# A trunk layer's output projection: four token tiles against eight weight chunks, or a block of seven half-size products

## The chip, the cores and the metric

The kernel runs on one core of one Trainium2 chip, in one launch. The metric is the device time of a run in microseconds; lower is better. Each engine has its own instruction queue: PE (matrix products, with its weight loads PEld), DVE (vector), ACT (scalar), POOL (GpSimd) and SP (issue of DMAs). POOL issues DMAs too, the accumulating ones among them.

## The reference

A two-layer encoder trunk on 512 tokens of width 1024, in float32. Cut to the token sublayer, where the change lies:

```python
for i in range(DEPTH):                                   # DEPTH = 2
    proj = x @ w_in[i]
    ...
    merged = sigmoid(gate_a) * (ya @ w_branch_a[i]) + sigmoid(gate_b) * (yb @ w_branch_b[i])
    y = merged @ w_out[i]                                # 512 x 1024 by 1024 x 1024
    x = layer_norm(DEEPNORM_ALPHA * x + y, ln1_g[i], ln1_b[i])
    ffn = conv_glu_ffn(x, w_up[i], conv_w[i], conv_b[i], w_down[i])
    ple = sigmoid(x @ w_ple_gate[i]) * (p[i] @ w_ple_proj[i])
    x = layer_norm(DEEPNORM_ALPHA * x + ffn + ple, ln2_g[i], ln2_b[i])
```

`layer_norm` subtracts the mean, multiplies by the reciprocal root of the variance plus 1e-5, then by a gain and adds a shift per channel.

## The kernel before

**Precision.** Every float32 operand of a matmul is split into a high part and a low part (`split`, line 753: ACT casts the high part, DVE subtracts it to get the low one). `mm3` issues three matmuls for one product: high by high, high by low, low by high. Weights come in packed chunks of 128 x 1024 (0.5 MB): an SP DMA into a raw buffer, then the split. `Stream` (line 870) holds the order in which chunks are used.

**Products in blocks of seven.** Most large products are already done as 2 x 2 blocks with seven half-size products instead of eight, named a, c, t1, t2, d, t3, t4. The weight sums that this needs are made by accumulating DMAs that POOL issues into the raw buffer (`Stream.add`); `block_items` (line 771) lists the chunks of a block: which chunk starts each buffer (`src`), which one is added to it (`plus`), and which item takes the buffer over (`nxt`). `vg_sums` (line 1345) makes the sums t1, t2, d, t3 of the activations: for each, two DVE operations of 128 x 512 form it, and ACT and DVE split it.

**The stage around the change,** in both layers alike:

- The merge (line 1884): for each of eight output blocks m, a product of the attention branch (bank gt) is multiplied by its gate, the other branch (gb) is added, both on DVE, and the result is split into `mt[m]`, channel-major, 512 tokens wide.
- The residual x is in four token tiles `xn` of 128 x 1024. In layer 1 it is the previous layer's normalised but unscaled output; `x_scale` (line 1729) multiplies it by the gain and adds the shift, eight DVE operations of 1024.
- The projection, `proj_ln` (line 1149, called in line 1940): the left column half of all four token tiles over eight K pieces (bank gn), each tile's result added to ALPHA times xn and its statistics taken; then the right half, in which the last four chunks are kept (`RESIDENT`) and the tiles are finished one after another. `ln_tile` (line 1140) normalises a tile with two DVE operations of 1024, which apply gain and shift; the reciprocal root is a tiny POOL operation (`rstd_of`).
- `done1(t)` (line 1922) turns a finished tile to channel-major: eight PE transposes (bank tr), copies by ACT into `xf`, and after every second tile the split into `x1t`. Tile t - 1 is turned behind tile t's matmuls; the last one at the mark T of the next stage.
- The next stage, `pg` (line 2155), runs the gate of the per-layer embedding as a block of seven (a, c, ...), mixed with blocks of the up-projection (0a, 0c, ...), in the order `PG`. It needs the turned tiles. `ple_gate` adds ALPHA times xn to the buffer R later; for two tiles ACT scales xn and a POOL DMA adds it.
- At the layer boundary the second layer norm is done in another way: `out_pair` (line 2375) turns two tiles that are normalised only, and ACT applies gain and shift per channel while it copies them out of PSUM.

**The order of the work.** From `VG_PLAN` in each layer to the last down segment, nothing is issued in program order except PE. `Program` records every operation; `_jobs`, `_dues` and `_order` model durations (`_costs`), due times and buffers, and fix the order of the other engines' queues and of the buffers; `_best` (called in `emit`) repeats this 12 times, raises the priority of the work that PE waits for in the model, and keeps the best order. The buffers are 30 units of 128 x 1024 shared by everything, 3 raw buffers, 3 pairs for split weights, 6 temporaries, 8 PSUM banks.

Of the kernel before, what the change touches and what calls it, by code (L numbers as in the profile page):

```python
# [9 lines left out]
F32 = mybir.dt.float32  # L10
# [31 lines left out]
XN_AT = (0, 0, 0, 0)  # L42
# [6 lines left out]
RESIDENT = {(l, c) for l in range(DEPTH) for c in range(68, 72)}  # L49
# [4 lines left out]
SENT = ((20, 24), (24, 32), (32, 36), (44, 52))  # L54

# [25 lines left out]
ROUNDS = 12  # L81
# [359 lines left out]

def _best(jobs, rounds=None):

    best, part = None, {}
    for j in jobs:
        j.boost = 0.0
    rounds = rounds or ROUNDS
    for r in range(rounds + 1):
        if r == rounds:
            if not part:  # L450
                break
            for j in jobs:
                if j.plan in part:
                    j.boost = part[j.plan][1][j]
# [3 lines left out]
        if end >= 1e9:  # L458
            for j in jobs:
                j.boost *= 0.6  # L460
            continue
        free, raise_, cost, now = 0.0, {}, {}, 0
        ends = {}
        for j, _ in order:
            ends.setdefault(round(j.done, 2), []).append(j)
        for j in sorted((j for j, _ in order if j.eng == "tensor"), key=lambda j: (j.start, j.seq)):
            gap, cur = j.start - free, j
            free = max(free, j.start + j.dur)
            now = j.plan or now
            cost[now] = cost.get(now, 0.0) + max(gap, 0.0)  # L470
            if gap < 0.08 or not j.plan:
                continue
            for _ in range(14):
                last = max(cur.after, key=lambda a: (a.done, a.seq), default=None)
                if last is None or cur.eng == "tensor" and cur.start - last.done > 0.3:
                    near = [x for d in range(-30, 1) for x in ends.get(round(cur.start + d / 100, 2), ()) if x.eng != "tensor"]
                    last = near[-1] if near and cur.eng == "tensor" else None
                if last is None or last.eng == "tensor":
                    break
                cur = last  # L480
                raise_[cur] = max(raise_.get(cur, 0.0), gap)
        for p, c in cost.items():
            if p and (p not in part or c < part[p][0]):
                part[p] = c, {j: j.boost for j in jobs if j.plan == p}
        if r == rounds:
            break
        for j, g in raise_.items():
            j.boost += 0.6 * g + 0.3
    for j, (a, b) in best[2].items():
        j.start, j.done = a, b  # L490
    return best[:2]
# [208 lines left out]
def trunk(tc, wpack, x_nat, x_tr, head, p_tr, rpb, decay, ln_par, ln_col, conv, cos_t, sin_t, dist, xi_d, zd, mask, ident_d, out):  # L700
# [5 lines left out]
    with ExitStack() as es:  # L706
# [50 lines left out]
        class Item:  # L757
# [7 lines left out]
            def __init__(self, kind, src, width, pool=None, plus=None, own=None):  # L765
                self.kind, self.src, self.width, self.pool, self.plus, self.own = kind, src, width, pool, plus, own
                self.raw = self.hl = None
                self.nxt = self.early = self.block = None
                self.sent = kind == "w" and any(a <= src[1] < b for a, b in SENT)

        def block_items(pos, held, early, n=2):
# [3 lines left out]
            for kind, src, plus in (("a", "a", None), ("c", "c", None), ("t1", None, "b"), ("t2", None, "d"),  # L775
                                    ("d", "d", None), ("t3", "b", "d"), ("t4", None, "c")):
                for j in range(n):
# [8 lines left out]
                    out.append(it)  # L786
            return out
# [82 lines left out]
        class Stream:  # L870


            def __init__(self):
                self.seq = []
                for l in range(DEPTH):
                    plain = lambda c: self.seq.append(Item("w", (l, c, 0, 1024), 1024, pool=up if (l, c) in RESIDENT else None))
# [17 lines left out]
            def add(self, it):  # L894
                l, c, o, w = it.plus
# [66 lines left out]
            def planned(self, it, pools=None):  # L962
# [31 lines left out]
                if it.nxt is not None:  # L994
                    it.nxt.raw = raw
                    self.add(it.nxt)
                prog.early = early
                return it.hl

            def raw_of(self, it):  # L1000
# [15 lines left out]
                if it.plus is not None:  # L1016
                    self.add(it)
# [86 lines left out]
        def gemm_n_tok(lh, nchunk, pss, first):  # L1104

            w = [ws.get(ahead=nchunk - 1 - c) for c in range(first, nchunk)]
            for t in range(4):
                if t >= len(pss):
                    pss.append(bank("gn"))
                for c in range(first, nchunk):  # L1110
                    gn_part(pss[t], lh, w[c - first], c, t, nchunk)
                yield t
# [36 lines left out]
        def proj_ln(lh, nchunk, z, add, g, b, done, follow):  # L1149

            st = [sp.tile([P, 2, 6], F32, tag="bn", name=nm("bn")) for _ in range(4)]

            def half(t, cb, ps):
                zz = z[t][:, cb * 512:(cb + 1) * 512]
                add(zz, ps)
                nc.vector.bn_stats(st[t][:, cb, :], zz)


# [1444 lines left out]
```

## Time and profile before

| | |
|---|---|
| time of three runs, us | 1654.0, 1654.13, 1655.08 (median 1654.13) |
| span of the profiled execution, us | 1652.4 |
| PE busy, us | 1639.2 (99%) |
| PE weight loads busy, us | 1461.2 (88%) |
| DVE busy, us | 1310.2 (79%) |
| ACT busy, us | 1001.6 (61%) |
| POOL busy, us | 276.9 (17%) |
| granted TensorE clock | 0.999 |
| DMA moved | 352.84 MB, mean 214 GB/s |
| first and last projection matmul of layer 0 and 1 | from 401.2 us to 1268.0 us |

The span runs from the first to the last instruction of one execution; the page gives no other time of it, and the runs' median lies 1.7 us above it. In rows of a group, x384 counts instructions and the two numbers behind the bar are busy us and mean ns of one; rows of one tile give min/median/max ns. Timelines give the start in us, then the duration, then engine, operation, and out<-in by tile names. All tensor operations carry line 264, where the recorded program is issued, so groups are told apart by their tiles: gn with mt is the projection, gt the merge's branch products, tr the transposes, lo<-raw the weight splits, rstd the reciprocal root.

### The profile page before, as it was taken

Reading aid. Unit: us, or ns where it says so; the run is one execution under the profiler, and the core shown is the slowest. Engines: PE = TensorE matmul, PEld = TensorE weight load, DVE = VectorE, ACT = ScalarE, POOL = GpSimd, SP = SyncE. Lnnn points to the kernel's source line nnn. Section 1 sums busy time; section 2 is a strip of 40 time slices with the busy share of each in tenths; the row PEclk is TensorE's granted clock in tenths of the full one; section 3 lists DMA queues with packets and bytes.
Section 4 is the critical chain, followed back from the end, with each engine's and each line's share of the span. In section 5 each row is a group of like instructions: output and inputs, shape, how many; then the busy total and the mean of one; then the engine's idle time right before and its main releaser. Section 6 shows DMA issues by size and latency. Waiting matters only on the chain.

```text
span 1652.4 us, 25561 instructions
## 1 busy us (share of the span) xinstructions
PE 1639.2 (99%) x9765; PEld 1461.2 (88%) x9765; DVE 1310.2 (79%) x1963; ACT 1001.6 (61%) x1495; POOL 276.9 (17%) x328
## 2 busy tenths in 40 slices
PE   9999999999999999999999999999999999999997
PEld 7889999888889898898888899998888898988986
DVE  6757999786878968768894579987689799687687
ACT  6665668953567556456484557788445674563564
POOL 1211113200211111112011102121002111111113
PEclk9999999999999999999999999999999999999999
DMA  8996669865699798888589657787755997989874
GB/s 306 270 245 172 154 159 220 202 180 194 167 298 244 196 282 201 245 252 205 182 253 248 166 143 184 187 202 181 208 214 170 288 267 203 261 187 276 230 173 128
DMA packets 104827, 352.84 MB, mean 214 GB/s; under 512 B 11904, under 2 KB 16512, under 8 KB 104704
## 3 DMA queue, kind: packets, MB, share of 16 engines
q0 software_dynamic: 41040, 147.34, 45.7%
q1 hardware_dynamic: 63664, 203.86, 33.7%
q8 instruction: 77, 1.26, 0.3%
q14 instruction: 46, 0.38, 0.1%
HBM read 323.89 MB, written 25.69 MB: 212 GB/s over the span
## 4 chain that ended last, share of the span: by engine, by line
PE 92%; DVE 4%; ACT 1%; DMA 1%; issue 1%; POOL 0%; DVEq 0%; POOLq 0%; ACTq 0%
PE u L264 30%; PE gt L264 23%; PE v L264 16%; PE gn L264 9%; PE w L264 7%; PE o L264 1%; PE x L264 1%; DVE lo L264 1%; PE ns L264 1%; PE na L264 1%; PE pt L264 1%; DMA gb_scr<-p 1%; PE tr L264 1%; DVE t L264 1%; DVE R L264 0%
## 5 line engine op out<-in xcount | busy, mean ns | idle before, releaser
L264 DVE TENSOR_TENSOR lo<-rawa,hi 128x1024 fp32r<-128x1024 f32 (+1 forms) x198 | 235.0, 1196 | 80.6 <-ACT hi L264 71.6
L264 POOL DMA_DIRECT2D rawa<-in_wpack x150 | 134.2, 911 | 955.5 <-DVE lo L264 750.1
L264 ACT CAST hi<-rawa 128x1024 fp32r<-128x1024 f32 (+1 forms) x198 | 202.4, 1032 | 104.2 <-DMA rawa<-in_wpack 85.2
L264 DVE TENSOR_TENSOR lo<-raw,hi 128x1024 fp32r<-128x1024 f32 (+1 forms) x159 | 191.0, 1205 | 38.3 <-ACT hi L264 38.1
L264 PE MATMUL gt<-x1t,hi 128*128 128x512 f32 x640 | 197.4, 390 | 0.0
L264 ACT CAST hi<-raw 128x1024 fp32r<-128x1024 f32 (+1 forms) x159 | 164.5, 1040 | 50.4 <-PE gn L264 14.7
L264 PEld LDWEIGHTS gt<-x1t,hi 128*128 128x128 f32 x640 | 118.8, 188 | 23.6
L264 PE MATMUL gt<-x1t,lo 128*128 128x512 f32 x320 | 124.5, 389 | 0.0
L264 PE MATMUL v<-sh,hi 128*128 128x256 f32 x288 | 81.9, 284 | 0.0
L264 PE MATMUL u<-sh,hi 128*128 128x256 f32 x288 | 81.8, 284 | 0.0
L264 PE MATMUL u<-xt,hi 128*128 128x256 f32 x448 | 81.7, 284 | 0.0
L264 PE MATMUL u<-sh,lo 128*128 128x256 f32 x288 | 81.5, 283 | 0.0
L264 PE MATMUL v<-sh,lo 128*128 128x256 f32 x288 | 81.5, 283 | 0.0
L264 PE MATMUL u<-sl,hi 128*128 128x256 f32 x288 | 81.5, 283 | 0.0
L264 PE MATMUL v<-sl,hi 128*128 128x256 f32 x288 | 81.5, 283 | 0.0
L264 ACT ACTIVATE uh<-u 128x512 f32<-128x512 f32 x60 | 35.7, 595 | 75.5 <-PE u L264 75.4
L264 PE MATMUL gn<-hi,mt 128*128 128x512 f32 x256 | 80.3, 391 | 0.0
L264 PE MATMUL gt<-ybt,hi 128*128 128x512 f32 x256 | 79.8, 393 | 0.0
L264 ACT ACT_TABLE_LOAD x49 | 62.9, 1283 | 18.5 <-DVE gg L264 9.7
L264 PE MATMUL v<-hi,sh 128*128 128x512 f32 x184 | 71.8, 390 | 0.1
L264 PE MATMUL v<-lo,sh 128*128 128x512 f32 x184 | 71.6, 389 | 0.0
L264 PE MATMUL v<-hi,sl 128*128 128x512 f32 x184 | 71.6, 389 | 0.0
(302 smaller groups left out, 4875.4 us busy)
## 6 DMA issues: line engine op xcount, KB each, us to landing
raw<-in_wpack SPq DMA_DIRECT2D x155, 512.0 KB, 6.8
rawa<-in_wpack POOLq DMA_DIRECT2D x144, 512.0 KB, 7.7
rawa<-in_wpack SPq DMA_DIRECT2D x48, 512.0 KB, 6.8
rawt<-in_wpack SPq DMA_DIRECT2D x48, 512.0 KB, 6.0
rawt<-in_wpack POOLq DMA_DIRECT2D x48, 512.0 KB, 9.8
hi<-in_wpack POOLq DMA_DIRECT2D x40, 512.0 KB, 7.1
lo<-in_wpack POOLq DMA_DIRECT2D x40, 512.0 KB, 6.4
sx<-s_scr SPq DMA_DIRECT2D x32, 512.0 KB, 9.4
```

Source lines behind the costliest of these rows:

```text
L264: r = o.call(*[real(x) for x in o.a], **{k: real(v) for k, v in o.k.items()})
```

## The change

The projection becomes a block of seven products over token halves, K halves and column halves, in the order `WO` = a, c, t1, t2, d, t3, t4a, T0, t4b (t4 is done in two halves, one token tile each; T0 turns tiles 0 and 1 between them). `vg_sums` makes the activation sums from the merged blocks; the first-half blocks `mt[0..3]` are split for the first 256 tokens only. Results are added into xn as they come, the first time with ALPHA times xn.

The chunks of w_out go through `block_items` with `mates`: t1, t2 and t3 get their weight sums by a POOL addition of 1024 columns from another raw buffer of the block (t3, d, d), and t3's buffer is summed once more behind d; t4's sum stays an accumulating DMA. Chunks are listed for this block and `RESIDENT` goes.

The merge's addition of the other branch, layer 1's `x_scale`, and gain and shift of layer norm 1 are POOL operations. `normed` only subtracts the mean and scales by the root, one DVE operation; `turned` (the boundary's code, now shared) applies gain and shift per channel by ACT, with columns from a new small input; the POOL operations make the scaled token-major xn for the later residual, from gain and shift that ACT has multiplied by ALPHA, so that the later scaling by ALPHA goes. At the mark T, tiles 2 and 3 are turned together. `_best` makes 60 rounds instead of 12: 12 that raise priorities as before, now for each of the two planned regions apart, then random variations of the best found, with a fixed seed.

```diff
-XN_AT = (0, 0, 0, 0)
+XN_AT = ("xn", "xn", "xn", "xn")
-RESIDENT = {(l, c) for l in range(DEPTH) for c in range(68, 72)}
+WO = ("a", "c", "t1", "t2", "d", "t3", "t4a", "T0", "t4b")
-ROUNDS = 12
+ROUNDS = 60
+WALK = 12
+SEED = 1
...
+            if mates:
+                of = lambda kind: [o for o in out if o.kind == kind]
+                for t1, t2, d, t3 in zip(of("t1"), of("t2"), of("d"), of("t3")):
+                    t1.mate, t2.mate, t3.mate, d.then = t3, d, d, t3
...
-                    for c in range(60, 72):
+                    for c in range(60, 64):
                         plain(c)
+                    pos = {(q, j): (l, 64 + 2 * i + j, 0, 1024) for i, q in enumerate("acbd") for j in range(2)}
+                    self.seq += block_items(pos, {}, VG_EARLY, mates=True)
...
             def add(self, it):
+                if it.mate is not None:
+                    self.raw_of(it.mate)
+                    nc.gpsimd.tensor_add(it.raw[:, :it.width], it.raw[:, :it.width], it.mate.raw[:, :it.width])
+                    return
...
-        def ln_tile(z, st, g, b, parts):
+        def normed(z, st):
             mv = small("mv", 2)
             nc.vector.bn_aggr(mv, st)
-            r = rstd_of(mv[:, 1:2], LN_EPS, 1)
-            nc.vector.scalar_tensor_tensor(z, z, mv[:, 0:1], g, op0=ALU.subtract, op1=ALU.mult)
-            for i in range(parts):
-                c = slice(i * D // parts, (i + 1) * D // parts)
-                nc.vector.scalar_tensor_tensor(z[:, c], z[:, c], r, b[:, c], op0=ALU.mult, op1=ALU.add)
+            nc.vector.tensor_scalar(z, z, mv[:, 0:1], rstd_of(mv[:, 1:2], LN_EPS, 1), op0=ALU.subtract, op1=ALU.mult)
...
-                        with kept():
-                            nc.vector.tensor_mul(xn[t], xn[t], xgb[0])
-                            nc.vector.tensor_add(xn[t], xn[t], xgb[1])
+                        nc.gpsimd.tensor_mul(xn[t], xn[t], xgb[0])
+                        nc.gpsimd.tensor_add(xn[t], xn[t], xgb[1])
...
-                nc.vector.tensor_add(sa, sa, gbu[m // 2][:, :, m % 2, :])
-                u = unit_r("mt")
-                split(v3(u[:, 0, :]), v3(u[:, 1, :]), sa)
+                nc.gpsimd.tensor_add(sa, sa, gbu[m // 2][:, :, m % 2, :])
+                if m < 4:
+                    if m % 2 == 0:
+                        mts = up.tile([P, 2, 2, 256], F32R, tag="u", name=nm("mt"))
+                    u = mts[:, m % 2]
+                    split(u[:, 0, :], u[:, 1, :], sa[:, 0, :])
+                else:
+                    u = unit_r("mt")
+                    split(v3(u[:, 0, :]), v3(u[:, 1, :]), sa)
...
+            for z in (g1, b1):
+                nc.scalar.activation(z, z, AF.Copy, scale=ALPHA)
...
             def done1(t):
+                turned(t, xn, gb1, xt, xf)
+                ts = slice(t * P, (t + 2) * P)
+                for k in range(4):
+                    split(xt[:, k:k + 5:4, 0, ts], xt[:, k:k + 5:4, 1, ts], xf[t // 2, k // 2][:, k % 2])
+                for i in (t, t + 1):
+                    nc.gpsimd.tensor_mul(xn[i], xn[i], g1)
+                    nc.gpsimd.tensor_add(xn[i], xn[i], b1)
...
+                def into(t, c, ps, op=ALU.add):
+                    z = xn[t][:, half[c]]
+                    if (t, c) in seen:
+                        nc.vector.tensor_tensor(z, z, ps, op)
+                        nc.vector.bn_stats(st[t][:, c, :], z)
+                    else:
+                        seen.add((t, c))
+                        nc.vector.scalar_tensor_tensor(z, z, ALPHA, ps, op0=ALU.mult, op1=op)
+                        if t > 1 and c == 0:
+                            nc.vector.bn_stats(st[t][:, c, :], z)
...
+                for _ in range(4):
+                    S.update(next(sg) or {})
+                for key in WO:
+                    if key[0] == "T":
+                        done1(int(key[1]))
+                        continue
...
+                    drain(products(key, ps, key in ("a", "c", "t1")))
+                    for i in range(2):
+                        if key in ("a", "c"):
+                            into(i, 0, ps[i])
+                        elif key in ("t2", "d"):
+                            into(i, 1, ps[i], ALU.subtract)
+                        else:
+                            into(2 + i, 1, ps[i], ALU.subtract)
+                    if key == "d":
+                        for i in range(2):
+                            normed(xn[i], st[i])
...
-                    nc.vector.scalar_tensor_tensor(R[t][:, c], xn[t][:, c], ALPHA, R[t][:, c], op0=ALU.mult, op1=ALU.add)
+                    nc.vector.tensor_add(R[t][:, c], R[t][:, c], xn[t][:, c])
...
-                    nc.scalar.activation(xn[t], xn[t], AF.Copy, scale=ALPHA)
                     nc.gpsimd.dma_start(R[t], xn[t], accum_op=ALU.add)
...
-                        done1(3)
+                        done1(2)
```

More of the change, by code (lines that the diff above doesn't have):

```diff
@@ L461, in _best @@
             continue
[L462 to L488, printed above, removed]
+        cost, raise_ = _gaps(order)
+        for p in plans:
+            now = {j: j.boost for j in jobs if j.plan == p}, raise_.get(p, [])
+            last[p] = now
+            if p not in part or cost.get(p, 0.0) < part[p][0]:
+                part[p] = (cost.get(p, 0.0),) + now
     for j, (a, b) in best[2].items():
@@ L1102, in gemm_n, with xf_at @@
                 yield
[L1104 to L1112, printed above, removed]
+        def xf_at(xf):
+            return lambda h, kp, q: xf[h, kp][:, :, q, :]
         def drain(g):
```

197 lines of the change are left out of this document (130 added, 67 removed).

## The prediction

> **What bounds the kernel now.** I read the page first: its busy times and the shares of the chain that ended last.
>
> ```profile
> span 1652.4 us, 25561 instructions
> PE 1639.2 (99%) x9765; PEld 1461.2 (88%) x9765; DVE 1310.2 (79%) x1963; ACT 1001.6 (61%) x1495; POOL 276.9 (17%) x328
> PE 92%; DVE 4%; ACT 1%; DMA 1%; issue 1%; POOL 0%; DVEq 0%; POOLq 0%; ACTq 0%
> ```
>
> PE is busy in all but 13.2 us of the span, and 92% of the chain is PE alone. So a matmul removed is worth its full step on PE, and whatever stops PE is worth its full length. I then asked how full the other engines are around the projection, with busy times by window: layer 0's projection lies in the first three, layer 1's in the fifth and sixth. The fourth is a stretch to compare with, the last is the kernel's tail. The columns are the window's length and the busy time (with instructions) of PE, its weight loads, DVE, ACT and POOL, then clock, DMA share and GB/s.
>
> ```profile
> 340.00:500.00 160.00, 160.00 (x838) 137.23 (x837) 120.93 (x183) 80.97 (x144) 19.72 (x21) 1.00 0.71 213
> 380.00:480.00 100.00, 100.00 (x492) 84.39 (x491) 83.11 (x115) 50.45 (x79) 13.03 (x13) 1.00 0.69 212
> 480.00:500.00 20.00, 20.00 (x130) 18.28 (x129) 9.06 (x9) 8.72 (x12) 4.39 (x5) 1.00 0.99 283
> 1000.00:1100.00 100.00, 98.95 (x821) 98.41 (x822) 96.58 (x186) 74.61 (x111) 22.62 (x28) 1.00 0.78 190
> 1160.00:1320.00 160.00, 158.66 (x822) 135.57 (x821) 129.51 (x191) 80.01 (x143) 20.02 (x21) 1.00 0.72 220
> 1200.00:1300.00 100.00, 98.66 (x485) 83.13 (x484) 92.74 (x126) 50.78 (x80) 13.84 (x13) 1.00 0.69 214
> 1600.00:1652.00 52.00, 43.95 (x194) 36.04 (x193) 44.08 (x66) 23.75 (x33) 13.96 (x13) 0.97 0.47 115
> ```
>
> The clock is full. PE has no hole in layer 0's stretch and 1.34 us of holes in layer 1's. DVE is the second engine: 83% busy in one, 93% in the other. POOL has room. Of PE's 13.2 us, 8.05 lie in the tail, which the change does not touch. What PE waited for, and the projection's place in the chain:
>
> ```profile
> PE tr L264 <- DVE xn L264: 1.3, 1, 1.3
> 379.79 21.55 PE gt L264 x95
> 401.34 32.65 PE gn L264 x144
> 447.76 8.32 PE u L264 x48
> ```
>
> The one wait near the projection is a transpose of xn behind the layer norm. The 144 matmuls in 32.65 us step at 0.227 us each. The last line is the next stage's first two products, a and 0a.
>
> **Part 1, the products.** All of the projection's matmuls, both layers:
>
> ```profile
> L264 PE MATMUL gn<-hi,mt x256: 388/389/481, 401.2 to 1268.0; 128*128 128x512 f32 x128
> L264 PE MATMUL gn<-lo,mt x128: 387/389/396, 401.4 to 1267.8; 128*128 128x512 f32 x128
> ```
>
> That is 384, so 192 a layer (4 token tiles, 2 column halves, 8 pieces of K, 3 terms). The block has seven products of 2 token tiles, 4 pieces of K and 3 terms: 168, of the same 512 columns. 24 fewer a layer are 24 x 0.227 = 5.45 us, 10.9 in all. The 32 transposes a layer stay.
>
> **Part 2, what DVE gains and loses.** Steps on DVE come from runs of one operation, where starts follow each other; the other rows are durations.
>
> ```profile
> 424.72 3.48 DVE L264 TENSOR_TENSOR lo<-rawa,hi 128x1024 fp32r<-128x1024 f32 x3
> 459.53 2.49 DVE L264 TENSOR_TENSOR x1t<-xf,x1t 128x512 fp32r<-128x512 f32 x4
> L264 DVE SCALAR_TENSOR_TENSOR xn<-xn,gn x16: 678/686/689, 419.1 to 1268.7; 128x512 f32<-128x512 f32 x16
> L264 DVE SCALAR_TENSOR_TENSOR xn<-xn,rstd,lnb x10: 736/1278/1285, 432.6 to 1276.4; 128x1024 f32<-128x1024 f32 x6, 128x512 f32<-128x512 f32 x4
> L264 DVE SCALAR_TENSOR_TENSOR xn<-xn,mv,lng x8: 1270/1274/1276, 430.8 to 1273.4; 128x1024 f32<-128x1024 f32 x8
> L264 DVE TENSOR_TENSOR xn<-xn,lng x4: 1216/1216/1217, 1227.1 to 1235.4; 128x1024 f32<-128x1024 f32 x4
> L264 DVE TENSOR_TENSOR xn<-xn,lnb x4: 1217/1224/1225, 1228.3 to 1241.6; 128x1024 f32<-128x1024 f32 x4
> 815.34 1.69 DVE L264 TENSOR_SCALAR R<-R,mv,rstd 128x1024 f32<-128x1024 f32 x2
> ```
>
> A 1024-wide subtraction takes 1.13 us of DVE (3.39 for three and a short drain), a 512-wide one 0.60, a 1024-wide normalisation by two scalars 0.8. Added per layer: 14 weight splits instead of 8, 6 x 1.13 = 6.8; sixteen operations for the sums t1, t2, d, t3 of the merged activations (8 that form them, 8 that split them), 16 x 0.60 = 9.6; 14 additions out of PSUM instead of 8 (the xn<-xn,gn row), 6 x 0.60 = 3.6. Taken away: 8 merge additions, 4.8; layer norm, two operations of 1.27 a tile against one of 0.8, 4 x (2.55 - 0.8) = 7.0; half of four mt splits, about 1.0 (an estimate from the 0.60). Net +7.2 a layer. In layer 1 the eight operations of the two 1024-wide rows by lng and lnb alone leave DVE as well, 8 x 1.14 = 9.1, so there it is -1.9.
>
> The stretch itself gets shorter, 100 to 94.55 us. DVE is then (83.1 + 7.2) / 94.55 = 95.5% busy in layer 0 and (92.7 - 1.9) / 94.55 = 96% in layer 1. The nearest row is 1000 to 1100: DVE at 96.6 us, PE lost 1.05. I take 1.05 a layer, 2.1 in all. Bounds: 1.3 won in all (layer 1's stretch has these holes today and they may close) and 3 a layer lost, if DVE cannot run ahead in the 11.2 idle us of 340 to 380 (the first row less the next two) for want of buffers.
>
> **Part 3, the turn to channel-major.** The new order is t3, t4a, T0, t4b, then the next stage's product a. T0 is 16 transposes of tiles 0 and 1, and the gain and shift are applied by ACT on the way out. The same turn stands today at the layer boundary:
>
> ```profile
> 810.68 0.68 DVE L264 TENSOR_TENSOR R<-R,v 128x512 f32<-128x512 f32 x1
> 824.28 1.91 PE L264 MATMUL tr<-ident,R 128*128 128x128 f32 x16
> 826.99 3.74 ACT L264 ACTIVATE xf<-tr,gb 128x256 f32<-128x256 f32 x8
> 830.60 2.20 ACT L264 CAST xt<-xf 128x512 fp32r<-128x512 f32 x4
> 832.32 2.49 DVE L264 TENSOR_TENSOR xt<-xf,xt 128x512 fp32r<-128x512 f32 x4
> ```
>
> In front of T0: from the addition at 810.68 to the end of the two normalisations at 817.03 are 6.35 us, and t3 and t4a cover 36 x 0.227 = 8.2. Hidden, with 1.8 us to spare; without the cover T0 would be 6.35 late, and with it a. Behind T0: t4b covers 12 x 0.227 = 2.7, so a starts 4.5 us after T0 does (1.75 for the transposes). In the order of these rows (all eight ACTIVATEs, then the casts) its first operand is ready 0.7 (four transposes and their way to ACT) + 3.74 + 0.55 (a cast) + 0.6 (a split) = 5.6 after T0's start, 1.1 late. Interleaved, a new operand comes every 2 x 0.47 + 0.55 = 1.5 us, the fourth at 0.7 + 6.0 + 0.6 = 7.3 against 7.9 needed; one foreign cast of 1 us between makes it 0.4 late. I take 1.0 a layer, 2.0 in all; bounds 0 and 3 a layer. Tiles 2 and 3 are turned after a and 0a, 8.3 us behind t4b: hidden like tiles 0 and 1.
>
> **Part 4, POOL.** New there per layer: six weight sums of 1024, eight merge additions of 512, and gain and shift of four tiles, eight of 1024; in layer 1 eight more of 1024 ahead of the projection.
>
> ```profile
> L264 POOL TENSOR_TENSOR R<-R,lng 128x1024 f32<-128x1024 f32 x1 | 2.4, 2409 | 0.0
> L264 POOL TENSOR_TENSOR R<-R,lnb 128x512 f32<-128x512 f32 x2 | 2.5, 1272 | 0.2 <-ACT R L264 0.2
> ```
>
> 6 x 2.41 + 8 x 1.27 + 8 x 2.41 = 43.9 us a layer, 63.2 in layer 1. With the 19.7 of 340 to 500 that is 64 to 83 of 154.5: POOL is no bound as an engine. Queued behind an addition are the reciprocal root of the norm and the issue of weight accumulations, each delayed by up to 2.41; the merge (mt of the eighth block is ready 0.7 + 1.27 + 0.62 + 0.69 = 3.3 us after its product and needed 8.9 us after it) and the sums lie under a and c. But POOL and DVE are not free of each other:
>
> ```profile
> 442.35 1.27 DVE L264 SCALAR_TENSOR_TENSOR xn<-xn,mv,lng 128x1024 f32<-128x1024 f32 x1
> 442.51 1.52 POOL L264 TENSOR_TENSOR rstd<-ve,mhalf 128x1 f32<-128x1 f32 x1 [4.02 <-DVE ve L264]
> 1634.67 0.68 DVE L264 TENSOR_TENSOR R<-R,v 128x512 f32<-128x512 f32 x1
> 1634.90 0.57 POOL L264 TENSOR_TENSOR rstd<-ve,mhalf 128x1 f32<-128x1 f32 x1 [12.09 <-DVE ve L264]
> 1637.79 0.69 DVE L264 TENSOR_TENSOR R<-R,w 128x512 f32<-128x512 f32 x1
> 1638.07 2.41 POOL L264 TENSOR_TENSOR R<-R,lng 128x1024 f32<-128x1024 f32 x1
> 1638.51 0.69 DVE L264 BATCH_NORM_STATS2 bn<-R 128x6 f32<-128x512 f32 x1
> ```
>
> The same root takes 0.57 us beside a DVE addition that reads PSUM (v), and 1.52 beside one whose two wide operands lie in SBUF: it ended 0.41 after that one did, so it waited for it. The trace has wide POOL additions only beside DVE work with at most one wide SBUF operand (w is PSUM), and neither was longer. What a wide addition does to a DVE operation with two is not shown. Bounds for the hot 94.55 us (weight sums and merge, 14.5 + 10.2 = 24.7 a layer): 0, and 24.7 if DVE stands still throughout. For the forecast I take 0: DVE is idle for 11.2 us before and 10.9 us (480 to 500) behind, and its PSUM additions and statistics, (14 + 8) x 0.6 = 13, can lie beside POOL's. Gain and shift of tiles wait in no hurry.
>
> The Trainium skill, "SBUF — State Buffer", section "Who interferes with whom", says that a DVE instruction with two SBUF inputs and a GpSimd instruction that reads SBUF exclude each other for the whole instruction, whichever starts first. The root's 1.52 us agrees for the one direction; the other is the first rival below.
>
> **The rest.** ACT gets 6 casts, 8 half casts and slower copies out of PSUM, about 13 us (an estimate from the boundary's rows) on 50.5 of 94.6: hidden. DMA gets two more accumulated chunks of 0.52 MB a layer, 4.9 us at 213 GB/s, at a share of 0.69: hidden. The longer search replans both layers: outside tail and projection PE has some 3.8 us of holes (13.2 - 8.05 - 1.34), so it can win at most that and may lose as much; I take 0.
>
> **The sum**, against the profiled span: 1652.4 - 10.9 + 2.1 + 2.0 = 1645.6. The runs' median, 1654.1, is 1.7 above that span (the page gives no other time of that execution), so 1647.3.
>
> **Rivals.** (1) POOL's additions hold DVE, and it is slower. If half of the 24.7 us falls on DVE work with two SBUF operands, DVE needs 90.3 + 12.3 = 102.6 us in 94.55, so 8 us a layer over: 1647.3 + 16 = 1663. The point from which it decides: 5.45 us a layer won less 2.05 spent leave 3.4, and DVE has 4 us left, so from about 7.5 us of held DVE a layer. For it: DVE at 96%, the 1.52 us root. Against it: idle DVE on both sides. Chance 0.30. (2) The turn eats it: a POOL addition of 2.41 ahead of each of the two roots uses up the 1.8 us in front of T0 (+3.0), and T0 to a takes its 3: with 1.05 for DVE, 7 us a layer against 5.45, 1654.1 - 10.9 + 14 = 1657; with one such delay, 1652. Against it: POOL's order can put the roots first. Chance 0.13, around no change. (3) The change does not do what it says: fourteen weight pairs, eight sums and the merged blocks do not fit ahead, weights come late, and only a few microseconds either way are left: 1654. Nothing in the trace shows free buffers. Chance 0.05.
>
> **Numbers.** The forecast has 0.52; its own range is 1640 (10.9 + 1.3, and 2 of the other holes) to 1651. A measurement of this kernel can tell about 0.2%, 3.3 us: faster means below 1650.8, slower above 1657.4. Faster 0.52 + 0.04 from (2) = 0.56; same 0.10 from (2) and (3); slower 0.30 + 0.04 = 0.34. Range for 8 in 10: 1641 to 1664, which takes in rival (1) at its price.
>
> **What would show it.** Right: 48 fewer PE matmuls, holes of PE in each projection under 3 us, DVE over 94% busy there. T0: a wait of a on DVE xt of about 1 us. Rival (1): DVE operations of 1.2 us drawn out to 2 or 3 beside POOL additions, and PE waiting for lo or the sums. Rival (2): PE tr waiting for xn, with rstd behind an addition. Wrong altogether: PE holes far from the projection.

## The result and the profile after

The changed kernel takes 1728.8 us, median of four runs (1727.27 to 1729.61), against 1654.22 us before (1654.0 to 1655.08). The ratio is 1.0449, interval 1.0437 to 1.0462: 74.6 us slower, where 1647.3 was forecast and 1664 was the end of the range. The first lines of the page after, the answer to those the prediction began with:

```profile
span 1727.2 us, 25613 instructions
...
PE 1654.4 (96%) x9717; PEld 1463.8 (85%) x9717; DVE 1397.3 (81%) x1985; ACT 1028.9 (60%) x1525; POOL 407.2 (24%) x384
...
PE 65%; DVE 11%; issue 7%; DMA 3%; POOL 1%; ACT 1%; DVEq 0%; POOLq 0%; ACTq 0%
```

PE has the 48 matmuls fewer that were promised (9717 against 9765), yet it is idle for 72.8 us of the span instead of 13.2. DVE has 22 instructions more and is busy for 87.1 us more. That is 4 us for each added instruction, where the rows of before in the prediction are 1.3 us and less: that is not more work, something makes the work longer. Where the time goes is read from busy times by window (columns as in the prediction: length, PE, PEld, DVE, ACT, POOL, then clock, DMA share, GB/s):

```profile
380.00:500.00 120.00, 91.61 (x395) 72.93 (x394) 114.56 (x116) 55.49 (x82) 60.23 (x35) 0.90 0.53 146
1200.00:1380.00 180.00, 149.93 (x689) 122.00 (x688) 161.76 (x183) 81.78 (x138) 92.06 (x48) 0.91 0.62 178
0.00:380.00 380.00, 377.43 (x2432) 343.01 (x2433) 297.43 (x504) 260.07 (x420) 69.22 (x83) 1.00 0.82 216
500.00:1200.00 700.00, 696.47 (x4286) 627.17 (x4285) 549.44 (x812) 439.19 (x638) 121.27 (x144) 1.00 0.82 212
```

The first two rows are the stretches around the two projections, with 28.4 and 30.1 us of idle PE; the other two are what lies ahead of and between them, with 2.6 and 3.5. The 8.3 that are left lie behind 1380 us, where the kernel before loses about as much in its tail. So the loss lies around the projections and nowhere else. The granted clock is 0.90 and 0.91 there, against 1.00 outside: the matmuls around the holes run slower too.

What PE waited for, over the whole run (us in total, times, longest):

```profile
PE gt L268 <- DVE x1t L268: 15.4, 2, 11.1
PE w L268 <- DVE mt L268: 7.7, 2, 5.2
PE u L268 <- DVE x1t L268: 7.1, 3, 3.7
PE w L268 <- DVE lo L268: 6.0, 2, 3.3
PE u L268 <- DVE lo L268: 5.6, 5, 2.5
```

Each of these, the five largest, is a wait for DVE: for turned activations, merge splits and weight splits. The longest hole is the place to see why DVE is late. The timeline of DVE there (start, duration, operation):

```profile
476.48 1.21 DVE L268 TENSOR_TENSOR lo<-raw,hi 128x1024 fp32r<-128x1024 f32 x1
477.62 11.69 DVE L268 TENSOR_TENSOR lo<-rawa,hi 128x1024 fp32r<-128x1024 f32 x2
489.23 1.28 DVE L268 TENSOR_TENSOR x1t<-xf,x1t 128x512 fp32r<-128x512 f32 x2
```

The same stretch on POOL, and on PE:

```profile
477.42 5.08 POOL L268 TENSOR_TENSOR xn<-xn,lng 128x1024 f32<-128x1024 f32 x2
482.26 4.81 POOL L268 TENSOR_TENSOR xn<-xn,lnb 128x1024 f32<-128x1024 f32 x2
```

```profile
481.50 0.39 PE L268 MATMUL gt<-x1t,hi 128*128 128x512 f32 x1
492.98 0.79 PE L268 MATMUL gt<-x1t,hi 128*128 128x512 f32 x1 [11.09 <-DVE x1t L268]
493.57 0.63 PE L268 MATMUL gt<-x1t,lo 128*128 128x512 f32 x1
```

Two subtractions, 2.3 us of work, take 11.69 us. They start 0.2 us after POOL starts gain and shift of two tiles (four operations), and end at 489.31. POOL has finished at 482.26 + 4.81 = 487.07, and from there it is 2.2 us: both ran only when POOL was through. Behind them in DVE's queue stand the splits of x1t that PE needs, so PE stands for 11.09 us. The last line shows the second loss: behind the hole a matmul takes 0.63 us instead of 0.39, at the lower clock.

This is rival (1) of the prediction. The rows of one tile (min/median/max in ns) show which DVE operations it befalls:

```profile
L268 DVE SCALAR_TENSOR_TENSOR xn<-xn,u x12: 664/675/689, 421.0 to 1332.9; 128x512 f32<-128x512 f32 x12
L268 POOL TENSOR_TENSOR xn<-xn,lng x12: 2408/2799/3381, 457.9 to 1349.8; 128x1024 f32<-128x1024 f32 x12
...
L268 DVE TENSOR_SCALAR xn<-xn,mv,rstd x8: 752/811/2898, 451.9 to 1342.4; 128x1024 f32<-128x1024 f32 x8
```

```profile
L268 DVE BATCH_NORM_STATS2 bn<-xn x16: 672/682/696, 439.1 to 1333.6; 128x6 f32<-128x512 f32 x16
```

The additions that read PSUM (u is a bank) never take over 0.69 us, whatever POOL does. The normalisation of a tile, one wide SBUF operand of 1024, takes 0.81 us or up to 2.9. The statistics of a tile, one SBUF operand of 512, are not drawn out, though two of them lie wholly inside POOL's operations. POOL loses as well: its operation of 2.41 takes 2.8 at the median.

### The profile page after: what moved, and what is told of

Same layout as the page of the kernel before. It is cut to its first block, busy times and chain, and to the rows that moved or that the text cites. A ratio compares the mean times of both kernels' runs of the same rounds, so it can differ in the third digit from the quotient of the medians.

```text
span 1727.2 us, 25613 instructions
## 1 busy us (share of the span) xinstructions
PE 1654.4 (96%) x9717; PEld 1463.8 (85%) x9717; DVE 1397.3 (81%) x1985; ACT 1028.9 (60%) x1525; POOL 407.2 (24%) x384
## 3 DMA queue, kind: packets, MB, share of 16 engines
q1 hardware_dynamic: 63952, 203.87, 32.6%
## 4 chain that ended last, share of the span: by engine, by line
PE 65%; DVE 11%; issue 7%; DMA 3%; POOL 1%; ACT 1%; DVEq 0%; POOLq 0%; ACTq 0%
PE u L268 20%; PE gt L268 19%; PE v L268 12%; PE w L268 5%; DVE lo L268 3%; PE gn L268 3%; DMA rawa<-in_wpack 2%; DVE s L268 1%; DVE sl L268 1%; PE x L268 1%; PE o L268 1%; PE ns L268 1%; PE na L268 1%; DVE xn L268 1%; PE pt L268 1%
## 5 line engine op out<-in xcount | busy, mean ns | idle before, releaser
L268 DVE TENSOR_TENSOR lo<-rawa,hi 128x1024 fp32r<-128x1024 f32 (+1 forms) x214 | 275.5, 1295 | 76.1 <-ACT hi L268 65.4
L268 POOL DMA_DIRECT2D rawa<-in_wpack x154 | 138.1, 914 | 834.1 <-DVE lo L268 600.4
L268 ACT CAST hi<-rawa 128x1024 fp32r<-128x1024 f32 (+1 forms) x214 | 218.9, 1032 | 100.4 <-DMA rawa<-in_wpack 80.5
L268 DVE TENSOR_TENSOR lo<-raw,hi 128x1024 fp32r<-128x1024 f32 (+1 forms) x151 | 186.3, 1237 | 26.9 <-ACT hi L268 26.8
L268 ACT CAST hi<-raw 128x1024 fp32r<-128x1024 f32 (+1 forms) x151 | 155.8, 1038 | 26.5 <-PE u L268 12.1
L268 PE MATMUL v<-hi,sh 128*128 128x512 f32 x216 | 86.5, 400 | 3.9 <-ACT hi L268 3.9
L268 PE MATMUL v<-hi,sl 128*128 128x512 f32 x216 | 86.1, 399 | 3.8 <-DVE sl L268 3.8
L268 PE MATMUL v<-lo,sh 128*128 128x512 f32 x216 | 85.9, 398 | 0.0
L268 PE MATMUL u<-lo,sh 128*128 128x512 f32 x200 | 79.0, 395 | 4.0 <-DVE lo L268 4.0
L268 PE MATMUL gt<-ybt,hi 128*128 128x512 f32 x256 | 79.8, 393 | 0.0
L268 PE MATMUL u<-hi,sh 128*128 128x512 f32 x200 | 78.7, 393 | 0.4 <-ACT hi L268 0.4
```

What stands on the lines that cost most here:

```text
L268: r = o.call(*[real(x) for x in o.a], **{k: real(v) for k, v in o.k.items()})
```

## The experiments

The leading theory, A in the expectations: wide POOL operations that read SBUF hold DVE, and nearly all of the 75 us is that. Against it stand the block itself (more DVE work at 95%, later weights, the turn), the mere length of POOL's queue, and the longer search with its other order. The kernels below tell these apart. In all edits `...` marks what is unchanged; runs of before beside them had medians of 1653.84 to 1654.13.

**Nothing wide on POOL.** The merge, `x_scale` and gain and shift go back to DVE, the weight sums to accumulating DMAs:

```diff
-                    self.seq += block_items(pos, {}, VG_EARLY, mates=True)
+                    self.seq += block_items(pos, {}, VG_EARLY)
...
-                        nc.gpsimd.tensor_mul(xn[t], xn[t], xgb[0])
-                        nc.gpsimd.tensor_add(xn[t], xn[t], xgb[1])
+                        nc.vector.tensor_mul(xn[t], xn[t], xgb[0])
+                        nc.vector.tensor_add(xn[t], xn[t], xgb[1])
...
-                nc.gpsimd.tensor_add(sa, sa, gbu[m // 2][:, :, m % 2, :])
+                nc.vector.tensor_add(sa, sa, gbu[m // 2][:, :, m % 2, :])
...
-                    nc.gpsimd.tensor_mul(xn[i], xn[i], g1)
-                    nc.gpsimd.tensor_add(xn[i], xn[i], b1)
+                    nc.vector.tensor_mul(xn[i], xn[i], g1)
+                    nc.vector.tensor_add(xn[i], xn[i], b1)
```

> The block of seven stays, and all its wide GpSimd work goes back: weight sums by accumulating DMAs, merge, layer 1's scale and shift, and gain and shift of layer norm 1 on VectorE. Theory A (wide GpSimd operations that read SBUF hold VectorE operations with two SBUF operands): the holes of PE go, VectorE has about 98 us of work in 94.5, so 1650, between 1643 and 1662. Rival B (the block itself: activation sums, turn, buffers): 1700 or more. Rival C (the new order of the queues is bad wherever the work runs): 1690 or more.

Measured: 1668.92 us (ratio 1.009, 1.0075 to 1.0105). Its engines, from the page, and its window in each layer:

```profile
PE 1636.6 (98%) x9717; PEld 1455.8 (87%) x9717; DVE 1348.7 (81%) x2025; ACT 1027.9 (62%) x1523; POOL 289.9 (17%) x344
```

```profile
380.00:480.00 100.00, 97.61 (x478) 81.69 (x477) 97.36 (x141) 61.16 (x90) 16.87 (x18) 1.00 0.84 228
...
1200.00:1300.00 100.00, 88.34 (x416) 73.15 (x415) 96.40 (x135) 56.21 (x84) 16.29 (x17) 0.95 0.78 222
```

60 of the 75 us are gone, and DVE is busy 48.6 us less than after although it has 40 operations more. But 15 us over before remain, more than theory A allowed for, at a DVE that is 97.4% busy in layer 0 and 96.4% in layer 1. PE's largest waits there still name DVE: 7.2 us for xn ahead of transposes, 4.1 for the low part of a sum (sl). This run changes the order and DVE's load along with POOL's, so it cannot say alone what held what.

**The same order, POOL writes only.** Each wide POOL operation is recorded with its operands, so that planner, order, buffers and waits stay as they are, but what runs is a fill of the output (so the weight sums, the merge's addition and gain and shift are not computed):

```diff
+        def wide(name, out, x, y):
+            prog.op("gpsimd", name, lambda o, a, b: tc.nc.gpsimd.memset(o, 0.5), (out, x, y), {})
...
-                nc.gpsimd.tensor_add(sa, sa, gbu[m // 2][:, :, m % 2, :])
+                wide("tensor_add", sa, sa, gbu[m // 2][:, :, m % 2, :])
```

and the same for the other three groups.

> The changed kernel in the same planned order, but each of the wide GpSimd additions and products writes a constant into its output tile and reads nothing (so weight sums, merge, and scale and shift are left out). Theory A: no SBUF read on GpSimd, so no VectorE operation is drawn out; 1645, between 1640 and 1655. Rivals B and C: the same order, block and dependencies, so 1715 to 1735.

Measured: 1649.04 us, ratio 0.9972 (0.9961 to 0.9983). Its span and engines, from the page, its two windows, and the timeline of the same two subtractions with the fills beside them:

```profile
span 1647.2 us, 25600 instructions
...
PE 1630.4 (99%) x9717; PEld 1451.7 (88%) x9717; DVE 1315.9 (80%) x1985; ACT 1027.8 (62%) x1525; POOL 324.8 (20%) x384
```

```profile
380.00:480.00 100.00, 99.77 (x492) 84.16 (x491) 92.60 (x133) 63.21 (x93) 29.80 (x37) 1.00 0.73 211
...
1200.00:1300.00 100.00, 97.90 (x488) 81.78 (x487) 90.85 (x132) 63.17 (x93) 40.47 (x45) 1.00 0.74 221
```

```profile
451.75 2.34 DVE L268 TENSOR_TENSOR lo<-rawa,hi 128x1024 fp32r<-128x1024 f32 x2
...
452.25 3.63 POOL L791 MEMSET xn<- 128x1024 f32 x4 [0.39 <-PE tr L268]
```

All 80 us are gone with the same order, the same products and the same 1985 DVE instructions, which now take 1315.9 us instead of 1397.3. The difference, 81.4 us, is a direct measure of how long the additions held DVE, since nothing of its work differs. The two profiled spans differ by 80.0 us (1727.2 less 1647.2): 56.0 of idle PE (72.8 less 16.8) and 24.0 of longer matmuls (busy 1654.4 less 1630.4 for the same 9717). The block, the order and the search are cleared of the loss.

The fills are not quite free for DVE. The two-operand subtractions beside them run at their usual 1.2 us, but two of the eight normalisations, which read one SBUF operand, take 1.70 and 1.42 us beside a fill where 0.81 is usual, 1.5 us in all. So 81.4 is low by about that much. The rows of the tile with fills:

```profile
L268 DVE TENSOR_SCALAR xn<-xn,mv,rstd x8: 759/810/1702, 435.5 to 1270.8; 128x1024 f32<-128x1024 f32 x8
```

**The same, with POOL as busy as after.** A fill of 1024 takes 0.95 us, an addition 2.41, so that run shortens POOL's queue too. Here two fills and a half stand for each operation:

```diff
+        def fill_slowly(o, a, b):
+            half = o[:, 0] if len(o.shape) == 3 else o[:, :o.shape[1] // 2]
+            for x in (o, o):
+                tc.keep_in_program_order(tc.nc.gpsimd.memset(x, 0.5))
+            return tc.nc.gpsimd.memset(half, 0.5)
```

> The write-only kernel again (weight sums, merge, scale and shift left out, planned order of the changed kernel), but with each wide GpSimd operation made of two and a half constant writes, so that it takes about as long as the addition did (2.4 us for 1024, 1.3 us for 512). Theory A (the SBUF reads hold VectorE): as the short writes, 1649 within 4. Rival D (it is the length of the GpSimd queue: its operations are late for those who wait for them, and the short writes only hid that): 1690 or more.

Measured: 1651.85 us, ratio 0.9989 (0.9979 to 0.9998). POOL is now busy for 76.40 us of 1200 to 1300, against 40.47 with single fills, and PE for 97.36:

```profile
1200.00:1300.00 100.00, 97.36 (x485) 80.96 (x484) 91.22 (x132) 62.99 (x93) 76.40 (x102) 1.00 0.72 211
```

So the length of the queue, with everything that is issued behind it, is worth 2.8 us of the 80. DVE is busy for 1315.9 us in this run as in the one before, so two and a half times as many fills hold it no longer. It is the reading of SBUF that costs, not the time on POOL.

**Each group by itself.** Four kernels, each with one group of real operations and the others as single fills: gain and shift of layer norm 1, the weight sums, the merge's addition, `x_scale`. The edit of the first, against the kernel with single fills:

```diff
-                    wide("tensor_mul", xn[i], xn[i], g1)
-                    wide("tensor_add", xn[i], xn[i], b1)
+                    nc.gpsimd.tensor_mul(xn[i], xn[i], g1)
+                    nc.gpsimd.tensor_add(xn[i], xn[i], b1)
```

> Planned order of the changed kernel; only gain and shift of layer norm 1 (16 operations of 1024) read SBUF on GpSimd, the other wide GpSimd operations write a constant (weight sums, merge, layer 1's scale and shift left out). In the changed kernel's trace these 16 held VectorE for about 33 us. Theory A: most of that becomes time of PE, 1672 to 1688. If single parts are harmless and only all of them together fill VectorE: 1649 to 1657.

> The same, only the 12 weight sums read SBUF on GpSimd (merge, both scales and shifts left out). Held in the changed kernel: about 20 us. Theory A: 1660 to 1670. If only the sum of the parts matters: 1649 to 1655.

> The same, only the 16 merge additions read SBUF on GpSimd (weight sums, both scales and shifts left out). Held in the changed kernel: about 13 us, but the kernel before took the same additions on GpSimd without loss (1654.5 against 1654.1). Theory A: 1649 to 1656.

> Planned order of the changed kernel; only layer 1's scale and shift of xn (8 operations of 1024) read SBUF on GpSimd, the other wide GpSimd operations write a constant (weight sums, merge, gain and shift of layer norm 1 left out). It is the last of the four parts: write-only 1649, layer norm +32.6, sums +17.4, merge +13.0, the changed kernel 1728.8. If the parts add up: 1666, between 1660 and 1671. If they overlap: 1650 to 1657.

The engine lines of the four pages, in this order:

```profile
PE 1640.6 (98%) x9717; PEld 1458.2 (87%) x9717; DVE 1348.3 (80%) x1985; ACT 1029.3 (61%) x1525; POOL 352.8 (21%) x384
```

```profile
PE 1636.9 (98%) x9717; PEld 1454.6 (87%) x9717; DVE 1334.8 (80%) x1985; ACT 1027.1 (62%) x1525; POOL 350.0 (21%) x384
```

```profile
PE 1637.1 (99%) x9717; PEld 1453.8 (88%) x9717; DVE 1329.4 (80%) x1985; ACT 1027.8 (62%) x1525; POOL 341.6 (21%) x384
```

```profile
PE 1638.2 (98%) x9717; PEld 1454.9 (87%) x9717; DVE 1330.1 (80%) x1985; ACT 1028.3 (62%) x1525; POOL 338.4 (20%) x384
```

DVE's work is the same in all of them, so its busy time less 1315.9 is what each group holds:

| real on POOL | operations x us alone | DVE held, us | time, us | ratio to before, interval | over 1649.04 |
|---|---|---|---|---|---|
| gain and shift | 16 x 2.41 = 38.6 | 32.4 | 1681.64 | 1.0171 (1.0155 to 1.0186) | 32.6 |
| weight sums | 12 x 2.41 = 28.9 | 18.9 | 1666.46 | 1.0077 (1.0062 to 1.0092) | 17.4 |
| merge | 16 x 1.27 = 20.3 | 13.5 | 1662.0 | 1.0048 (1.0033 to 1.0063) | 13.0 |
| `x_scale`, layer 1 | 8 x 2.41 = 19.3 | 14.2 | 1664.57 | 1.0063 (1.0048 to 1.0078) | 15.5 |
| sum of the four | 107.1 | 79.0 | | | 78.5 |
| all (after) | 107.1 | 81.4 | 1728.8 | 1.0449 (1.0437 to 1.0462) | 79.8 |

The parts add up to the whole within 1.3 us, and each us of held DVE costs about one us of time. The merge was expected at 1649 to 1656 and missed that. Gain and shift, which the prediction had put aside, are the largest term.

**One operand instead of two.** If only the two-operand form held DVE, gain and shift could be written otherwise. The 16 operations of layer norm 1 become multiplications by a constant (so gain and shift are not applied), the rest are single fills:

```diff
+        def one_read(name, out, x, y):
+            prog.op("gpsimd", name, lambda o, a, b: tc.nc.gpsimd.tensor_scalar_mul(o, a, 1.25), (out, x, y), {})
...
-                    nc.gpsimd.tensor_mul(xn[i], xn[i], g1)
-                    nc.gpsimd.tensor_add(xn[i], xn[i], b1)
+                    one_read("tensor_mul", xn[i], xn[i], g1)
+                    one_read("tensor_add", xn[i], xn[i], b1)
```

> As the run with layer norm 1 alone on GpSimd (1681.6), but its 16 operations multiply xn by a number: one SBUF operand read instead of two (gain, shift, weight sums, merge, layer 1's scale and shift left out). If any wide GpSimd read of SBUF holds VectorE: they are shorter, so 1658 to 1680, and VectorE operations are drawn out by the length of theirs. If only the second operand does it: 1647 to 1654.

Measured: 1667.15 us, ratio 1.008 (1.0063 to 1.0097), 18.1 over the fills. DVE beside the POOL operations in the timeline, and all 16 in the rows of the tile:

```profile
453.81 6.30 DVE L268 TENSOR_TENSOR lo<-rawa,hi 128x1024 fp32r<-128x1024 f32 x2
...
454.55 8.93 POOL L794 TENSOR_SCALAR xn<-xn 128x1024 f32<-128x1024 f32 x3
```

```profile
L794 POOL TENSOR_SCALAR xn<-xn x16: 2767/3426/3822, 439.1 to 1294.5; 128x1024 f32<-128x1024 f32 x16
```

One operand still holds DVE, for somewhat over half as long in sum (busy 1333.8 on its page, 17.9 held against 32.4). The operation takes no less time on POOL, though it was expected to be shorter. A second operand is not needed for the holding; other one-operand forms were not run.

**One group in the kernel before.** The merge's addition moved to POOL in before, nothing else:

```diff
-                nc.vector.tensor_add(sa, sa, gbu[m // 2][:, :, m % 2, :])
+                nc.gpsimd.tensor_add(sa, sa, gbu[m // 2][:, :, m % 2, :])
```

> The kernel before, with only the merge's eight additions a layer moved to GpSimd (replanned). Theory A: 16 additions of 1.27 us, beside VectorE at 85%, are held or hold in part: 1657 to 1668, with VectorE operations of 0.68 or 1.22 us drawn out by about 1 us beside them. Rival B: 1654, no change beyond 3 us.

Measured: 1654.46 us, ratio 1.0003 (0.9994 to 1.0012): nothing, and theory A's 1657 to 1668 missed. The engines, from the page, and the timeline of one addition with the split beside it:

```profile
PE 1639.0 (99%) x9765; PEld 1461.0 (88%) x9765; DVE 1307.1 (79%) x1947; ACT 1001.6 (61%) x1495; POOL 302.0 (18%) x344
```

```profile
389.66 1.67 POOL L264 TENSOR_TENSOR ga<-ga,gb 128x512 f32<-128x512 f32 x1 [1.24 <-DVE ga L264]
...
390.10 2.31 DVE L264 TENSOR_TENSOR lo<-raw,hi 128x1024 fp32r<-128x1024 f32 x1
```

The holding is there (2.31 us for a split of 1.22). DVE loses 16 operations of 0.60, 9.6 us, and its busy time falls by only 3.1, so 6.5 were held. But DVE is still 3.1 better off. The 13.0 us that the merge costs in the changed kernel are counted from fills, with the additions on neither engine; against 9.6 us on DVE, its 13.5 held are 3.9 more. So the same move relieves DVE here and loads it there, and the price of one us per us belongs to the changed kernel, not to the chip. That it needs a DVE without slack is a reading: no run varies the slack alone.

**The search alone.** Before, with the changed `_best` and ROUNDS = 60, WALK = 12, SEED = 1:

```diff
-ROUNDS = 12
+ROUNDS = 60
+WALK = 12
+SEED = 1
```

> The kernel before with the new search of 60 rounds alone. Theory A and rival B: 1654 within 4. Rival C (the search, random variations included, gives orders that are worse on the chip than in its model): 1670 or more.

Measured: 1652.49 us, ratio 0.9991 (0.9982 to 1.0). Its window 1200 to 1300 has PE at 99.70 us where before had 98.66. At most a small gain, at the edge of what can be told.

**A version that could win?** The block with nothing wide on POOL, `x_scale` on DVE at the start of the merge, and DVE relieved of the splits of the c and d weights (their low part made by ACT and an accumulating DMA: 4 x 1.13 = 4.5 us a layer):

```diff
-XN_AT = ("xn", "xn", "xn", "xn")
+XN_AT = (0, 0, 0, 0)
...
-SENT_CD = ()
+SENT_CD = ((64, 72),)
```

with the edits of the first experiment; and a second one with `x_scale` left on POOL but its loads asked for 45 us ahead, to let it run where DVE is idle:

```diff
+                    early, prog.early = prog.early, 45 if l else prog.early
...
+                    prog.early = early
```

> A version meant to beat both kernels: the block of seven with no wide work on GpSimd (as the first experiment, 1669), and to relieve VectorE the c and d weights of the block get their low part from ScalarE and an accumulating DMA instead of a VectorE subtraction (four a layer, 4.5 us); layer 1's scale and shift at its old place on VectorE. Theory A with VectorE as the bound: 1669 less up to 9, so 1652 to 1664; if VectorE has room again, 1645 to 1650.

> The same, but layer 1's scale and shift on GpSimd, with the loads of xn asked for 45 us ahead, so that its eight operations fall where VectorE is half idle (1160 to 1200 in the kernel before). Theory A: GpSimd reads cost nothing where VectorE has nothing to do, and 9 us leave VectorE: 1646 to 1656. If the operations land in the hot stretch all the same: 1660 to 1672.

Measured: 1670.65 us (1.0099, 1.0082 to 1.0116) and 1684.12 us (1.0179, 1.0164 to 1.0194). Both lie above everything that was expected of them, and neither beats before or the first experiment. The windows of the first:

```profile
380.00:480.00 100.00, 95.17 (x448) 78.56 (x448) 91.21 (x129) 58.99 (x85) 22.53 (x25) 0.98 0.92 250
1200.00:1300.00 100.00, 92.12 (x428) 75.90 (x427) 90.86 (x128) 53.25 (x82) 21.77 (x24) 0.95 0.89 244
```

DVE is relieved in the stretch (90.86 where the first experiment had 96.40), but over the whole run by only 4.6 us (1344.1 against 1348.7 busy) where 9.0 were meant, and the time is no shorter. `x_scale` has another place here than in the first experiment, so the two differ in more than the splits. The DMA share is 0.9 now; whether the transfers set the time was not followed, and PE's largest waits still name DVE (6.8 us for sl, 4.9 for lo, 4.0 for xn). In the second the operations came early, but in the merge, where DVE was not idle either. DVE and POOL there:

```profile
1236.34 13.87 DVE L268 TENSOR_TENSOR sl<-s,sh 128x512 fp32r<-128x512 f32 x1
```

```profile
1236.55 5.32 POOL L268 TENSOR_TENSOR xn<-xn,lng 128x1024 f32<-128x1024 f32 x2
1241.20 5.24 POOL L268 TENSOR_TENSOR xn<-xn,lnb 128x1024 f32<-128x1024 f32 x2
...
1246.40 3.25 POOL L268 TENSOR_TENSOR xn<-xn,lnb 128x1024 f32<-128x1024 f32 x1
```

And PE's longest wait:

```profile
PE w L268 <- DVE mt L268: 13.4, 1, 13.4
```

One subtraction of 0.68 us stands for 13.87 us behind five POOL operations in a row, and PE stands 13.4 us for a merge split behind it. No complete version beat before by more than the 1.6 us of the longer search.

## Why the prediction was wrong

**The products (Part 1)** were right in number: 48 fewer. With the fills PE's busy time falls by 8.8 us (1639.2 to 1630.4) against 10.9 worked out; the missing 2 was not followed.

**DVE's work (Part 2)** was right in its sum: 7.2 in layer 0 less 1.9 in layer 1, so 5.3; with the fills DVE is busy 1315.9 - 1310.2 = 5.7 more. The squeeze, 1.05 us a layer at a DVE 95.5 to 96% busy, was not tested by that run: DVE is 92.6 and 90.9% busy in its windows, and PE lacks 0.2 and 2.1 of 100 there, where before lacks 0 and 1.3. Where DVE did come to 97.4 and 96.4%, in the first experiment, PE lacks 2.4 and 11.7. So one window at 96.6% was no price for another: at about the same busy share the loss was anything from 1 to 12 us.

**The turn (Part 3)** was put at 2.0; with the fills PE waits 0.6 us for x1t on bank u and 0.4 for xn ahead of a transpose. Rival (2) needed a late root. After, transposes wait 3.6 us for xn in all, with the fills 0.4, and in the first experiment, with nothing wide on POOL, 7.2: xn is late where DVE is behind, whether it is held or has more to do.

**POOL (Part 4)** is the step that failed: "For the forecast I take 0". The runs show 81.4 us of held DVE there, and 79.8 us of time. Three things in it were wrong.

First, what was counted. "Gain and shift of tiles wait in no hurry" is true of who needs them, and beside the point: not being urgent does not keep an operation out of the hot stretch. These work in place and take no buffer; by the code nothing in the planner delays them. In the trace the first of each pair of tiles starts within 1.3 us of the pair's last transpose. They and `x_scale` were left out of the bound of 24.7 a layer, and are 46.6 of the 79.0 us held.

Second, how much of it falls on DVE. The "idle 11.2 us before and 10.9 behind" were counted as if POOL would use them, and PSUM work as if it would lie beside POOL's. The PSUM work is indeed untouched, as the rows show, but 81.4 of 107.1 us of POOL's wide work held DVE, 76%. This is also where the offload turns around: merge, gain and shift and `x_scale` on POOL hold DVE for 13.5 + 32.4 + 14.2 = 60.1 us, while on DVE they take 1348.7 - 1315.9 = 32.8 (first experiment, 40 operations more). They cost DVE nearly twice as much by being taken off it.

Third, the slack. Rival (1) let DVE absorb 4 us a layer and charged half of 24.7: 16 us. The two groups that it did count, sums and merge, hold 32.4 and cost 30.4. So almost nothing was absorbed. The longest hole suggests why, though no run isolates it: DVE's slack is an average over a window, and an operation held for 10 us delays at once all that stands behind it in the queue.

So rival (1) had the mechanism and its signs (drawn-out operations, PE waiting for lo and the sums), with a chance of 0.30, and a size of 16 us for one of 80. The trace of before held the evidence for the one direction, the root of 1.52 us; the sentence of the Trainium skill ("SBUF — State Buffer", section "SBUF: two separate sides") that the exclusion lasts for the whole instruction, whichever starts first, is borne out in the other direction by 2.34 us with fills against 11.69 with additions. Charged at full length to all of POOL's new work, 107.1 us, that rule gives an estimate of 1647.3 + 107.1 = 1754 as the bound, where the working had 24.7 a layer and so 1697.

**The rest:** the search was put at 0 and measures -1.6; ACT and DMA were put at hidden, and with the fills no wait of PE over 0.2 us names either.

Without the holding the change is worth 1654.1 - 1649.0 = 5.1 us with short fills, and 2.0 with POOL about as busy as in after (1653.84 before beside it, less 1651.85); the forecast of 1647.3 was 1.7 and 4.6 too good for these. What stays open: why four and five POOL operations in a row hold one DVE operation throughout at 477 and at 1236, while at other places the two engines take turns; and what makes up the 15 us by which the block with everything on DVE stays above before. By the prediction's own terms DVE's work does not fit there: 90.3 + 13.9 = 104 us in layer 0 and 90.8 + 23.0 = 114 in layer 1 for a stretch of 94.55, and PE's waits name DVE. But the version that took some of it away was no faster, so DVE as the cause is argued, not shown.

## What to carry to other kernels

Where VectorE is the second bound, a wide GpSimd operation that reads SBUF is to be charged to VectorE too, urgent or not, with its full length as the upper end (76% of it was held here, 6.5 of 20.3 us in the kernel before), and compared with what the operation would take on VectorE itself; here that was 60 us against 33. To measure it, keep the order and replace the operations by fills of their outputs: VectorE's busy time, with its instructions unchanged, then gives the held time, less the little that the fills hold themselves. A planner that models the two engines as independent cannot see this and can place such work where it does harm, so the holding belongs in its costs.

## What the hardware showed beyond that

A run of GpSimd operations can hold one VectorE operation through all of them (13.87 us for 0.68, behind five), though elsewhere they alternate. After, at 411 to 421 us, DVE and then POOL:

```profile
412.16 3.37 DVE L268 TENSOR_TENSOR lo<-rawa,hi 128x1024 fp32r<-128x1024 f32 x1
415.46 2.82 DVE L268 TENSOR_TENSOR mt<-ga,mt 128x512 fp32r<-128x512 f32 x1
418.20 2.86 DVE L268 TENSOR_TENSOR s<-ga,ga 128x512 f32<-128x512 f32 x1
```

```profile
411.65 2.79 POOL L268 TENSOR_TENSOR rawa<-rawa,raw 128x1024 f32<-128x1024 f32 x1
414.41 3.32 POOL L268 TENSOR_TENSOR rawt<-rawt,raw 128x1024 f32<-128x1024 f32 x1
417.69 2.81 POOL L268 TENSOR_TENSOR rawa<-rawa,raw 128x1024 f32<-128x1024 f32 x1
```

Here each DVE operation waits for one addition and passes between two. One thing in the rows goes with the difference. Where DVE passed, the next addition starts as the one ahead ends (411.65 + 2.79 = 414.44, next at 414.41). Where one DVE operation was held throughout, the next starts earlier: 477.42 + 5.08 = 482.50 with the next at 482.26, and 1236.55 + 5.32 = 1241.87 with the next at 1241.20. In all the runs the overlap is 0.23 to 0.67 us in the nine cases of the second kind and at most 0.06 in the others. With the multiplication by a constant, though, records overlap by 0.7 us and DVE passes all the same. No run varied this, so it is a mark of such places and not their cause.

Single-operand work is not always spared: a normalisation of 0.81 us took up to 2.9, and a GpSimd multiplication by a constant held VectorE too; but the statistics, one operand of 512, kept to 0.70. Fills of GpSimd drew out no two-operand operation of VectorE, only the normalisation, up to 1.70 us. VectorE operations that read PSUM were never drawn out in the changed kernel.
